# A decoder step on one core: the second MLP tile's relu, square and split issued behind the next pair's first copy

## Chip, core and metric

The kernel runs on one NeuronCore of one Trainium2 chip. The time is the device time of one execution in microseconds (us); of several executions the median is given. The engines are called PE (the matrix engine; PEld its weight loads), DVE (the vector engine), ACT (the scalar engine), POOL and SP (which issues the loads and stores). Each engine works through its own list of instructions in the order in which the program issued them, and waits where an instruction needs another engine's result.

## What is computed

One layer of a hybrid decoder for 512 prompt rows and 8 sample rows together, T = 520 columns in the kernel's transposed layout, all in fp32. The part that matters here is the MLP at its end and the final norm:

```python
u2 = rmsnorm(x, norm2_g) * (1 + sc2) + sh2
hmid = jnp.square(jax.nn.relu(u2 @ w_mlp1))
x = x + g2 * (hmid @ w_mlp2)
...
y_prompt = rmsnorm(yp, norm_f_g)
y_sample = rmsnorm(ys, norm_f_g)
```

The model width is 1024, the MLP's inner width 4096. Everything ahead of it (modulation, input projection, short convolution, state-space scan, output projections) is the same in both kernels.

## The kernel before

**Split products.** Each fp32 operand is written as a high and a low part (hi and lo for activations, wh and wl for weights), and a product is the sum of three matmuls (hi by wh, lo by wh, hi by wl). ACT makes the high part by a copy (`a_copy`, L140), and DVE the low part by a subtraction (`tt`, L128) that needs the copy. All matmuls stand at L143.

**Three groups of pairs.** The first of four quarters of `w_mlp1` is done plainly. In the other three quarters the output tiles (128 rows by T columns each) are made two at a time by `seven` (L1337): with the tokens and the 1024 inputs in halves, a Strassen-like scheme needs seven products instead of eight. A quarter has four such pairs (below pair 1 to pair 4 of a group), and after them come the windows of `w_mlp2` for that quarter, the first two by `two` (L1320), the others by `one` (L1306). The last two windows of the kernel have their own code.

**A pair.** The products p0 to p6 have 12 matmuls each and go to three accumulation banks in the order y, x, w, y, x, w, x. A bank is written again by a later product, so that what must be read of it in between has to be read first. `after(p)` (L1349) issues this reading: behind p0 ACT copies y into `s1` (the first half of tile `su`); behind p1 and p2 DVE adds into `u2_` (the second half of `su`) and `s15` (shown as `s`); behind p3 ACT writes relu of y into the first half of the first output tile `r0`; behind p4 DVE writes half of the second output tile `r1`; behind p5 DVE writes the rest of `r0`, and `squares` (relu, square, copy to hi) issues three ACT instructions on it; behind p6 DVE writes the rest of `r1`, then makes lo of `r0` (`m1_lo`, L790), and `squares` follows on `r1`. Both output tiles appear as `relu` in rows of the profile. What is put into the list `later` is issued in the next pair, in `two` after its first product.

**Weights of a pair.** `split_s` (L292) makes four pairs of wh and wl per pair of tiles, t = 0 to 3, from a loaded weight tile wt and from sums of its quarters, `ss`, that DVE adds first. wh of the sum at t = 2 is issued ahead of p0, its wl ahead of p1; t = 3 ahead of p2 and p3; t = 0 and 1 of the next pair ahead of p4 to p6. So on ACT the two copies from `ss` stand ahead of the copy of y.

**The final norm.** In the last quarter `m2_evac` (L803) finishes x tile by tile: DVE adds the product into `x` (rs, rs, then L131 and a copy at L706), ACT and DVE add its square, and `finish_tile` (L856) transposes the tile on PE (`pt`, `pts`) and multiplies the transposes by the norm's weights on DVE (five `yo` instructions a tile). The place of `finish_tile` is set by `at(q, w, ...)` and `run`: behind quarter q of window w. `mid` is 1 and `end` is 3.

Of the kernel before, what the change touches and what calls it, by code (L numbers as in the profile page):

```python
# [72 lines left out]
def tile_hybrid_step(  # L73
# [32 lines left out]
    def act(name, dtype=F32):  # L106
        return ap.tile([P, SLOT], dtype, name=nm(name), tag="act", bufs=NSLOT)
# [7 lines left out]
    def aux(name):  # L115
        return pp.tile([P, 512], F32, name=nm(name), tag="aux", bufs=4)
# [10 lines left out]
    def tt(out, in0, in1, op):  # L127
        V.tensor_tensor(out=out, in0=in0, in1=in1, op=op)  # L128
# [10 lines left out]
    def a_copy(out, in_, func=AF.Copy, **kw):  # L139
        S.activation(out=out, in_=in_, func=func, **kw)  # L140

    def mm(out, lhsT, rhs, start=True, stop=True, **kw):
        PE.matmul(out, lhsT=lhsT, rhs=rhs, start=start, stop=stop, **kw)  # L143
# [105 lines left out]
    hooks, mid, end = {}, 1, 3  # L249
# [99 lines left out]
    def at(q, w, fn, *args):  # L349
        hooks.setdefault(4 * w + q, []).append((fn, args))  # L350

    def run(w, q):
        while 4 * w + q in hooks:
            for fn, args in sorted(hooks.pop(4 * w + q), key=lambda h: PLAN["order"].get(h[0].__name__, 0)):
                fn(*args)
# [273 lines left out]
    def add_square(acc, t, first, n=T):  # L629
        d = acc if first else act("sqt")  # L630
        a_copy(d[:, 0:n], t[:, 0:n], AF.Square)
        if not first:
            tt(acc[:, 0:n], acc[:, 0:n], d[:, 0:n], ALU.add)
# [67 lines left out]
    def residual(x_, xo, ps, prm, o):  # L701
        t = small([P, NS], "rs")
        tt(t, ps[:, 1, NP - TH:TH], msm(prm, o), ALU.mult)
        tt(t, t, xo[:, NP:T], ALU.add)
        stt(halves(x_[:, 0:T]), ps[:, :, 0:TH], mp(prm, o), halves(xo[:, 0:T]))
        V.tensor_copy(out=x_[:, NP:T], in_=t)  # L706
# [83 lines left out]
    def m1_lo(r, hi, lo):  # L790
        tt(lo[:, 0:T], r[:, 0:T], hi.bitcast(F32)[:, 0:T], ALU.subtract)
        hm.append((hi, lo))
# [10 lines left out]
    def m2_evac(ps, w, o, half):  # L803
        residual(x2[o], x2[o], ps, 5, o)
        if half:
            if o == 0:
                sqf.insert(0, act("sqf"))
            add_square(sqf[0], x2[o], o == 0)
            if o == KT - 3:
                V.memset(vf, 1.0)  # L810
                at(end, w + 1, row_means, sqf, 1.0 / D, vf)
            at(mid if o else end, w + 1, finish_tile, o)

    sqf = []
    vf = const([P, 5], "vf")
# [100 lines left out]
    for f in range(4):  # L916
        for q in range(8):
            if f and q % 2 == 0:
                pairs.add(len(wins))
            win("m1", 0, 1024 * f + 256 * (q // 2), q % 2, lambda: u2, None if f else m1_evac, n1=SLOT - TH)  # L920
        twos.add(len(wins))
        for k in range(KT):
            win("m2", D * f, 256 * (k // 2), k % 2, lambda f=f: hm[8 * f:8 * f + 8],
                lambda ps, w, k=k, f=f: m2_evac(ps, w, k, f == 3))
# [95 lines left out]
    def splits_to(n, whole=True):  # L1020
        while state["split"] < len(units) and state["split"] <= n:
            u_ = units[state["split"]]
            split_w(*u_) if len(u_) == 1 else split_s(*u_)
            state["split"] += 1
        while whole and rests:
            rests.pop(0)()
# [273 lines left out]
    later = []  # L1300

    def evac(n):
        if wins[n][3]:
            wins[n][3](ps_of.pop(n), n)
# [32 lines left out]
    def seven(n):  # L1337
        y, x, w = (aux(z)[:, 0:TH] for z in ("yb", "xb", "wb"))
        banks = (y, x, w, y, x, w, x)
        su, s15, r0, r1 = act("su"), act("s15"), act("relu"), act("relu")  # L1340
        s1, u2_ = su[:, 0:TH], su[:, TH:T]
        hl = [(act("hi", F32R), act("lo", F32R)) for _ in range(2)]

        def squares(r, hi, c0):
            a_copy(r[:, c0:T], r[:, c0:T], AF.Relu)
            a_copy(r[:, 0:T], r[:, 0:T], AF.Square)
            a_copy(hi[:, 0:T], r[:, 0:T])

        def after(p):  # L1349
            if p == 0:  # L1350
                a_copy(s1, y)
                while later:
                    later.pop(0)()
                evac(n - 1)
            elif p == 1:
                tt(u2_, x, s1, ALU.add)
            elif p == 2:
                tt(s15[:, 0:TH], w, s1, ALU.add)
            elif p == 3:
                a_copy(r0[:, 0:TH], y, AF.Relu)  # L1360
            elif p == 4:
                tt(r1[:, TH:T], x, s15[:, 0:TH], ALU.add)
            elif p == 5:
                tt(r0[:, TH:T], w, u2_, ALU.add)
                squares(r0, hl[0][0], TH)
            else:
                tt(r1[:, 0:TH], x, s1, ALU.add)
                m1_lo(r0, *hl[0])
                squares(r1, hl[1][0], 0)
                later.append(lambda: m1_lo(r1, *hl[1]))  # L1370

        for p in range(7):
            splits_to(unit_of[n] + p // 2 + 2, p % 2 == 1)
            (hi, lo), c = splits[n, p // 2], 4 * (p % 2)
            for k in range(4):
                xh, xl = terms[p][k]
                for i, (w_, x_) in enumerate(((hi, xh), (hi, xl), (lo, xh))):
                    mm(banks[p], w_[:, c + k, :], x_, p < 3 and k == 0 and i == 0, k == 3 and i == 2,
                       skip_group_check=True)
            after(p)  # L1380
            run(n + p // 4, p % 4)
        splits_to(unit_of[n] + 5)
        run(n + 1, 3)
# [61 lines left out]
```

## Time and profile before

| | |
|---|---|
| median of 3 runs | 1161.29 us (1161.14 to 1161.82) |
| the profiled execution's own time | 1163.04 us |
| its span in the profile | 1161.3 us |
| PE busy | 1128.1 us |
| DVE busy | 809.0 us |
| ACT busy | 497.5 us |
| four pairs and what follows them until the next group | 872.60 to 962.60, 962.60 to 1052.50 |
| the third group and the end | 1052.50 to 1161.3 |

The span is what the profile shows between the first and the last instruction; the profiled execution took 1.7 us more around it. A row of the timeline gives the start, the length, the engine, the line, the operation with its output and inputs, and in brackets how long the engine stood idle ahead of it and which instruction ended that.

### The profile page before, as it was taken

The numbers are of one execution on the slowest core, as the hardware profiler recorded it, in microseconds if no ns is written. First come the engines' busy times: TensorE is split into PE (matmuls) and PEld (weight loads), VectorE is DVE, ScalarE is ACT, GpSimd is POOL, SyncE is SP. The second block draws the span as 40 slices with busy tenths as digits, with TensorE's granted clock in tenths as the row PEclk, the third lists the DMA queues.
The fourth block names the chain that finished last, engine by engine and source line by source line (L and its number), as shares of the span: only waits on it lengthen the run. The fifth ranks groups of instructions, "written<-read, shape, count | busy, mean of one in ns | idle before, by whom it ended". The sixth has DMA issues, their size and how long they took to land.

```text
span 1161.3 us, 22937 instructions
## 1 busy us (share of the span) xinstructions
PE 1128.1 (97%) x9554; PEld 1092.7 (94%) x9554; DVE 809.0 (70%) x1566; ACT 497.5 (43%) x780; POOL 46.1 (4%) x85
## 2 busy tenths in 40 slices
PE   6999999999999999999999999999999999999997
PEld 5798999999998888999999999999999999999996
DVE  5677888678888587888567334578777647657764
ACT  5456555455552222234443222345536515524622
POOL 3001111011110000000000000003000000000000
PEclk9999999999999999999999999999999999999999
DMA  9924333333348996567563243332222332332302
GB/s 280 326 74 132 114 115 96 94 112 114 114 147 292 324 329 199 178 187 212 171 230 101 95 165 124 114 124 97 81 96 73 109 110 73 109 110 73 104 7 74
DMA packets 137747, 164.96 MB, mean 142 GB/s; under 512 B 7144, under 2 KB 107961, under 8 KB 137636
## 3 DMA queue, kind: packets, MB, share of 16 engines
q1 hardware_dynamic: 137116, 162.85, 42.9%
q8 instruction: 75, 1.23, 0.4%
q0 software_dynamic: 528, 0.66, 0.2%
q14 instruction: 28, 0.23, 0.1%
HBM read 145.26 MB, written 18.45 MB: 141 GB/s over the span
## 4 chain that ended last, share of the span: by engine, by line
PE 83%; ACT 6%; DVE 6%; DMA 3%; issue 1%; SPq 1%; ACTq 0%; DVEq 0%
PE ps L143 72%; DMA wa<-in_w_ada_dram 2%; ACT wh L140 2%; DVE wl L128 2%; ACT relu L140 2%; PE xb L143 1%; PE pada L143 1%; PE pyd L143 1%; PE pst L143 1%; PE pyo L143 1%; PE yb L143 1%; ACT hi L140 1%; PE wb L143 1%; DVE cv L131 1%; DVE ss L128 1%
## 5 line engine op out<-in xcount | busy, mean ns | idle before, releaser
L143 PE MATMUL ps<-hi,wh 128*128 128x260 f32 (+2 forms) x2432 | 501.7, 286 | 2.4 <-ACT cv L140 1.1
L143 PE MATMUL ps<-lo,wh 128*128 128x260 f32 (+2 forms) x2432 | 493.3, 283 | 1.7 <-DVE lo L128 1.4
L143 PE MATMUL ps<-hi,wl 128*128 128x260 f32 (+2 forms) x2432 | 491.0, 282 | 0.0
L143 PEld LDWEIGHTS ps<-hi,wh 128*128 128x128 f32 x2432 | 375.2, 188 | 18.1 <-issue 13.6
L143 PEld LDWEIGHTS ps<-lo,wh 128*128 128x128 f32 x2432 | 376.5, 188 | 3.3 <-DVE lo L128 3.3
L143 PEld LDWEIGHTS ps<-hi,wl 128*128 128x128 f32 x2432 | 376.0, 188 | 0.0
L140 ACT ACTIVATE wh<-wt 128x1024 fp32r<-128x1024 f32 (+1 forms) x191 | 183.1, 960 | 318.3 <-PE ps L143 301.9
L128 DVE TENSOR_TENSOR wl<-wt,wh 128x1024 fp32r<-128x1024 f32 (+1 forms) x191 | 210.4, 1103 | 66.2 <-ACT wh L140 66.2
L131 DVE SCALAR_TENSOR_TENSOR cv<-raw,par,cv 128x511 f32<-128x511 f32 (+2 forms) x72 | 54.0, 750 | 10.9 <-ACT cv L140 9.0
L128 DVE TENSOR_TENSOR rs<-ps,mod 128x8 f32<-128x8 f32 x40 | 6.6, 164 | 62.4 <-PE ps L143 62.4
L140 ACT ACTIVATE wh<-ss 128x512 fp32r<-128x512 f32 x48 | 28.7, 621 | 31.7 <-PE ps L143 26.0
L143 PE MATMUL xb<-hi,wl 128*128 128x260 f32 x144 | 40.8, 283 | 0.0
L143 PE MATMUL xb<-hi,wh 128*128 128x260 f32 x144 | 40.7, 283 | 0.0
L143 PE MATMUL xb<-lo,wh 128*128 128x260 f32 x144 | 40.5, 282 | 0.0
L140 ACT ACTIVATE relu<-relu 128x520 f32<-128x520 f32 (+2 forms) x56 | 29.4, 525 | 20.0 <-DVE relu L128 19.2
L425 POOL TENSOR_SCALAR_AFFINE_SELECT seg<-seg 128x512 f32<-128x512 f32 x32 | 24.9, 801 | 299.6 <-DVE seg L128 243.9
L143 PE MATMUL yb<-hi,wh 128*128 128x260 f32 x96 | 28.1, 293 | 8.2 <-ACT su L140 8.2
L140 ACT ACT_TABLE_LOAD x27 | 34.6, 1283 | 2.9 <-DVE cv L131 1.7
L140 ACT ACTIVATE cv<-cv 128x520 f32<-128x520 f32 x24 | 15.3, 639 | 43.1 <-DVE cv L131 43.1
L128 DVE TENSOR_TENSOR wl<-ss,wh 128x512 fp32r<-128x512 f32 x48 | 31.8, 683 | 0.0
L143 PE MATMUL pada<-wa,cT 128*32 128x128 f32 (+1 forms) x384 | 29.0, 400 | 1.1 <-DMA wa<-in_w_ada_dram 0.9
L131 DVE SCALAR_TENSOR_TENSOR x<-ps,mod,x 128x520 f32<-128x520 f32 (+1 forms) x34 | 24.7, 727 | 5.7 <-PE ps L143 4.6
(312 smaller groups left out, 1332.9 us busy)
## 6 DMA issues: line engine op xcount, KB each, us to landing
wt<-in_w_in_dram SPq DMA_DIRECT2D x38, 1024.0 KB
wt<-in_w_mlp_dram SPq DMA_DIRECT2D x32, 1024.0 KB
wa<-in_w_ada_dram SPq DMA_DIRECT2D x96, 256.0 KB
acb<-ascr SPq DMA_DIRECT2D x32, 256.0 KB
hn<-in_state_ssm_dram SPq DMA_DIRECT2D x32, 256.0 KB
out_dram<-hn SPq DMA_DIRECT2D x32, 256.0 KB
wt<-in_w_b_out_dram SPq DMA_DIRECT2D x8, 1024.0 KB
gscr<-sg SPq DMA_DIRECT2D x16, 260.0 KB
```

The source lines that it names most:

```text
L128: V.tensor_tensor(out=out, in0=in0, in1=in1, op=op)
L131: V.scalar_tensor_tensor(out=out, in0=in0, scalar=scalar, in1=in1, op0=op0, op1=op1)
L140: S.activation(out=out, in_=in_, func=func, **kw)
L143: PE.matmul(out, lhsT=lhsT, rhs=rhs, start=start, stop=stop, **kw)
L425: G.affine_select(out=sv, in_=sv, pattern=[[0, NC], [1, P]], compare_op=ALU.is_ge, fill=-1e30, base=0, channel_multiplier=-1)
```

## The change

In `seven` the relu, the square and the copy to hi of the second output tile are no longer issued at the end of their pair. They go into `later`, and the next pair issues them behind its copy of y (`s1`). The matching `m1_lo` moves from behind p0 of the next pair to behind p2. In `two`, which follows pair 4, both are still issued behind the first product. In `m2_evac` the transposes of the first output tile (o = 0) move from the end of window w + 1 to the middle of window w + 2, where those of o = 1 already stand.

```diff
@@ m2_evac
-            at(mid if o else end, w + 1, finish_tile, o)
+            at(mid, w + (1 if o else 2), finish_tile, o)
@@ seven: after(p)
             if p == 0:
                 a_copy(s1, y)
-                while later:
+                if later:
                     later.pop(0)()
                 evac(n - 1)
             elif p == 1:
                 tt(u2_, x, s1, ALU.add)
             elif p == 2:
                 tt(s15[:, 0:TH], w, s1, ALU.add)
+                while later:
+                    later.pop(0)()
...
             else:
                 tt(r1[:, 0:TH], x, s1, ALU.add)
                 m1_lo(r0, *hl[0])
-                squares(r1, hl[1][0], 0)
+                later.append(lambda: squares(r1, hl[1][0], 0))
                 later.append(lambda: m1_lo(r1, *hl[1]))
```

On ACT, at the seam of pair 2 and pair 3 of the first group, this stood before. The two `wh<-` rows at the top are t = 1 of pair 3, the relu row of 520 columns is relu and square of the second tile of pair 2:

```order
L140 ACTIVATE wh_10825<-ss_10786 128x512
L140 ACTIVATE wh_10825<-wt_10434 128x512
L140 ACTIVATE relu_10714<-relu_10714 128x520 x2
L140 ACTIVATE hi_10717<-relu_10714 128x520
L140 ACTIVATE wh_10865<-ss_10861 128x512
L140 ACTIVATE wh_10865<-ss_10863 128x512
L140 ACTIVATE su_10853<-yb_10850 128x260
L140 ACTIVATE wh_10898<-wt_10434 128x512
```

and this stands now:

```order
L140 ACTIVATE wh_10825<-ss_10786 128x512
L140 ACTIVATE wh_10825<-wt_10434 128x512
L140 ACTIVATE wh_10862<-ss_10858 128x512
L140 ACTIVATE wh_10862<-ss_10860 128x512
L140 ACTIVATE su_10850<-yb_10847 128x260
L140 ACTIVATE relu_10711<-relu_10711 128x520 x2
L140 ACTIVATE hi_10714<-relu_10711 128x520
L140 ACTIVATE wh_10897<-wt_10434 128x512
```

Relu, square and hi have moved behind three instructions, the two copies from `ss` and the copy of y.

On DVE at the same seam (the two sums `ss` for t = 2, then what follows them) this stood before:

```order
L128 TENSOR_TENSOR ss_10861<-wt_10434 128x512
L128 TENSOR_TENSOR ss_10863<-wt_10434,ss_10788 128x512
L128 TENSOR_TENSOR lo_10718<-relu_10714,hi_10717 128x520
L128 TENSOR_TENSOR wl_10866<-ss_10861,wh_10865 128x512
L128 TENSOR_TENSOR wl_10866<-ss_10863,wh_10865 128x512
L128 TENSOR_TENSOR su_10853<-xb_10851,su_10853 128x260
L128 TENSOR_TENSOR s_1406_10854<-wb_10852,su_10853 128x260
L128 TENSOR_TENSOR wl_10899<-wt_10434,wh_10898 128x512
```

and this stands now:

```order
L128 TENSOR_TENSOR ss_10858<-wt_10434 128x512
L128 TENSOR_TENSOR ss_10860<-wt_10434,ss_10788 128x512
L128 TENSOR_TENSOR wl_10863<-ss_10858,wh_10862 128x512
L128 TENSOR_TENSOR wl_10863<-ss_10860,wh_10862 128x512
L128 TENSOR_TENSOR su_10850<-xb_10848,su_10850 128x260
L128 TENSOR_TENSOR s_1406_10851<-wb_10849,su_10850 128x260
L128 TENSOR_TENSOR lo_10715<-relu_10711,hi_10714 128x520
L128 TENSOR_TENSOR wl_10898<-wt_10434,wh_10897 128x512
```

The lo of the second tile has moved behind four instructions and stands now right ahead of the wl of t = 3; the set of instructions is the same.

On DVE in the last quarter (x_8879 is tile o = 0, x_8953 is o = 1) this stood before:

```order
L128 TENSOR_TENSOR wl_13305<-wt_12928,wh_13304 128x1024
L128 TENSOR_TENSOR yo_13320<-pt_13325,gbc_9771 128x128
L128 TENSOR_TENSOR yo_13321<-pt_13325,gbc_9771 128x128
L128 TENSOR_TENSOR yo_13322<-pt_13325,gbc_9771 128x128
L128 TENSOR_TENSOR yo_13323<-pt_13325,gbc_9771 128x128
L128 TENSOR_TENSOR yo_13324<-pts_13326,gbc_9771 8x128
L128 TENSOR_TENSOR rs_13353<-ps_13248,mod_5769 128x8
L128 TENSOR_TENSOR rs_13353<-rs_13353,x_1134_8953 128x8
L131 SCALAR_TENSOR_TENSOR x_1134_8953<-ps_13248,mod_5769,x_1134_8953 128x520
```

and this stands now:

```order
L128 TENSOR_TENSOR wl_13305<-wt_12925,wh_13304 128x1024
L128 TENSOR_TENSOR rs_13336<-ps_13248,mod_5769 128x8
L128 TENSOR_TENSOR rs_13336<-rs_13336,x_1134_8953 128x8
L131 SCALAR_TENSOR_TENSOR x_1134_8953<-ps_13248,mod_5769,x_1134_8953 128x520
```

The five `yo` of the first tile have moved behind the finishing of x of the second; on PE the first tile's five transposes now stand right ahead of the second's.

## Rows read from the trace of the kernel before

**Rows 1.** The page, part 1: busy us (share), instructions.
```profile
PE 1128.1 (97%) x9554; PEld 1092.7 (94%) x9554; DVE 809.0 (70%) x1566; ACT 497.5 (43%) x780; POOL 46.1 (4%) x85
```

**Rows 2.** What PE waited for: us in total, times, longest.
```profile
PE yb L143 <- ACT su L140: 8.2, 9, 0.9
...
PE pt L864 <- DVE x L131: 1.8, 2, 1.5
```

**Rows 3.** Stretches: length, busy PE, PEld, DVE, ACT, POOL, clock, DMA.
```profile
872.60:916.55 43.95, 41.21 (x340) 40.59 (x339) 35.28 (x66) 28.17 (x53) 0.00 (x0) 1.00 0.28 95
916.55:962.60 46.05, 46.05 (x385) 45.96 (x385) 23.57 (x46) 12.26 (x17) 0.00 (x0) 1.00 0.29 94
```

**Rows 4.** Timeline of PE: first matmuls of p0 and p3, pair 3.
```profile
893.88 0.28 PE L143 MATMUL yb<-hi,wh 128*128 128x260 f32 x1
...
899.27 0.39 PE L143 MATMUL yb<-hi,wh 128*128 128x260 f32 x1 [0.92 <-ACT su L140]
```

**Rows 5.** Timeline of DVE from pair 2's end through pair 3 into pair 4.
```profile
892.78 0.42 DVE L128 TENSOR_TENSOR relu<-wb,su 128x260 f32<-128x260 f32 x1
...
895.03 0.70 DVE L128 TENSOR_TENSOR lo<-relu,hi 128x520 fp32r<-128x520 f32 x1 [0.52 <-ACT hi L140]
...
896.85 0.68 DVE L128 TENSOR_TENSOR ss<-wt 128x512 f32<-128x512 f32 x1
897.45 0.68 DVE L128 TENSOR_TENSOR ss<-wt,ss 128x512 f32<-128x512 f32 x1
898.05 0.69 DVE L128 TENSOR_TENSOR lo<-relu,hi 128x520 fp32r<-128x520 f32 x1
898.67 1.28 DVE L128 TENSOR_TENSOR wl<-ss,wh 128x512 fp32r<-128x512 f32 x2
899.87 0.42 DVE L128 TENSOR_TENSOR su<-xb,su 128x260 f32<-128x260 f32 x1
...
900.54 0.68 DVE L128 TENSOR_TENSOR wl<-wt,wh 128x512 fp32r<-128x512 f32 x1
...
904.00 0.42 DVE L128 TENSOR_TENSOR relu<-wb,su 128x260 f32<-128x260 f32 x1
...
913.72 0.43 DVE L128 TENSOR_TENSOR relu<-xb,s 128x260 f32<-128x260 f32 x1 [1.27 <-PE xb L143]
```

**Rows 6.** Timeline of ACT at the seam of pairs 2 and 3.
```profile
894.35 0.64 ACT L140 ACTIVATE hi<-relu 128x520 fp32r<-128x520 f32 x1
...
895.94 1.29 ACT L140 ACTIVATE relu<-relu 128x520 f32<-128x520 f32 x2
897.27 0.64 ACT L140 ACTIVATE hi<-relu 128x520 fp32r<-128x520 f32 x1
897.82 1.13 ACT L140 ACTIVATE wh<-ss 128x512 fp32r<-128x512 f32 x2
898.85 0.36 ACT L140 ACTIVATE su<-yb 128x260 f32<-128x260 f32 x1
```

**Rows 7.** The chain that ended last: start, us, what; pair 4 from p3, then `two`.
```profile
910.50 1.73 PE yb L143 x12
...
916.55 3.48 PE ps L143 x29
```

**Rows 8.** Timeline of PE where the second tile's transposes wait.
```profile
1110.95 0.41 PE L143 MATMUL ps<-hi,wl 128*128 128x260 f32 x2
1112.84 0.66 PE L864 MATMUL pt<-ident,x 128*128 128x128 f32 x4 [1.48 <-DVE x L131]
...
1113.36 0.48 PE L143 MATMUL ps<-hi,wh 128*128 128x260 f32 x2
```

**Rows 9.** Timeline of DVE in the same stretch.
```profile
1110.65 0.88 DVE L128 TENSOR_TENSOR yo<-pt,gbc 128x128 f32<-128x128 f32 x4
...
1111.64 0.14 DVE L128 TENSOR_TENSOR rs<-ps,mod 128x8 f32<-128x8 f32 x1
```

## The prediction

> **What bounds the kernel now.** I read the page first: PE is busy for 97% of the span, DVE for 70%, ACT for 43% [rows 1]. So only time in which PE stands still can be won, and the waits of PE say where that is: the largest entry is nine waits for the copy of y, `su`, 8.2 us together [rows 2]. Three groups with three seams each make nine. The table of stretches shows the same: a group of four pairs takes 43.95 us with PE busy for 41.21, the `w_mlp2` windows behind it take 46.05 and PE is busy for all of them [rows 3]. What is lost in the pairs is therefore not caught up later, and what is won there is kept.
>
> Then the timelines of one seam, to see who sets the pace. PE starts p0 of pair 3 at 893.88 and p3 at 899.27 [rows 4]. A product takes (916.55 - 910.50 - 1.73) / 3 = 1.44 us [rows 7], so p3 was due at 893.88 + 3 x 1.44 = 898.20 and came 1.07 us late, behind `su`.
>
> PE waits, but it is not the engine that sets the period. DVE works from lo of `r0` at 895.03 to the relu row of p5 at 904.00 without one idle gap, sixteen instructions, of which I show some [rows 5]; that is 8.97 us. The remaining 2.25 us, from that relu row (892.78) to lo of `r0` (895.03), is the way over ACT: relu, square and hi of `r0`, for whose end DVE waits 0.52 us [rows 5]. Together 904.00 - 892.78 = 11.22 us, the period of the pairs in the middle. PE needs 7 x 1.44 = 10.08 for a pair. So the middle pairs run on a ring of DVE work and ACT's three instructions on `r0`; PE's wait for `su` is where PE is held back to this period. Only in pair 4, where no `ss` of a next pair is made, does DVE catch up: its sum behind p4 waits 1.27 us for PE [rows 5]. From there PE's p3 sets the end of the group.
>
> **The change at a seam, step by step.** I count from S, the start of the first `ss` for t = 2 (896.85 in pair 3). Before, the second `ss` starts at S + 0.60, lo of `r1` at S + 1.20, the two wl at S + 1.82, `u2_` at S + 3.02, wl of t = 3 at S + 3.69 (900.54) [rows 5]. On ACT relu and square of `r1` start at S - 0.91 and take 1.33 to hi, hi starts at S + 0.42, the two wh from `ss` at S + 0.97, `su` at S + 2.00, and PE's p3 at S + 2.42 [rows 4, 6]. DVE had lo of `r1` ready to go: its hi had ended at S + 1.06.
>
> Now ACT reaches the two wh from `ss` first, and is there too early: it is past hi of `r0` and the wh of t = 1 at 895.94, S - 0.91 [rows 6], and the sums are not made yet. A hand-over between ACT and DVE costs 0.04 (hi of `r0` ends at 894.99, its lo starts at 895.03) [rows 5, 6]. So wh of the first sum starts at S + 0.68 + 0.04 = 0.72, that of the second at S + 0.60 + 0.68 + 0.04 = 1.32. Half of the 1.03 from 897.82 to 898.85 is 0.52, so `su` starts at S + 1.84 instead of 2.00 [rows 6]. **PE's p3 comes 0.16 us earlier, not 1.07.** The removed 1.88 us of ACT work (895.94 to 897.82) mostly gives way to a wait for DVE's sums.
>
> Relu and square of `r1` follow `su`, 0.36 - 0.09 = 0.27 behind its start (ACT's instructions without a wait overlap by 0.09: 897.27 + 0.64 against 897.82), at S + 2.11. hi starts 1.33 later, at S + 3.44, and ends at S + 4.08 [rows 6]. lo of `r1` starts at S + 4.12. It takes 0.62 to the next instruction (898.05 to 898.67), and wl of t = 3 starts at S + 4.74 instead of S + 3.69 [rows 5]. **DVE loses 1.05 us at each seam.** Two wl, `u2_` and `s15` end at about S + 3.3, since lo of `r1` is gone from ahead of them; DVE then stands for some 0.8 us in front of lo, with wl of t = 3, the next pair's `ss`, the sum behind p4 and everything up to p5's relu queued behind it. No work covers this: the same sixteen instructions lie between lo of `r0` and p5's relu, and the ring is now 11.22 + 1.05 = 12.27 us.
>
> **Sum over a group.** Pair 1 has no predecessor and does not change. The seams of pairs 1 and 2 and of pairs 2 and 3 delay the next pair's S by 1.05 each. In pair 4 p3 comes 2 x 1.05 - 0.16 = 1.94 us later. There DVE is 3 x 1.05 = 3.15 late against PE's 1.94, 1.21 more, and it waited 1.27 for PE: the third loss just disappears in that wait. From p3 to the first product of `two` PE needs the same four products, 910.50 to 916.55 [rows 7]. In `two` the late hi and lo are wanted only with its seventh product of 1.44, some 8 us in, so nothing waits for them. A group is 1.94 us longer, three groups 5.8 us.
>
> **The transposes.** Before, PE ends the first half of the second window at about 1111.2, stands 1.48 us for x of tile o = 1, and starts its transposes at 1112.84 [rows 8]. DVE was late for that x by the five `yo` of tile 0, 1110.65 to 1111.64, 0.99 us [rows 9]. With them behind it, x comes 0.99 earlier, and the transposes start at 1111.85. Tile 0's five transposes (1112.84 to 1113.36 is what five take, 0.52 [rows 8]) are only issued later on PE, so PE reaches the wait at the same time. Gain 0.99 us; the bounds are 0 (if DVE's later work fills it) and the 1.65 from 1111.19 to 1112.84. The two tiles' ten `yo` then stand together, 2 us of DVE in a window of some 6 us, which holds.
>
> **Sum.** +5.8 - 1.0 = +4.8 us. The profiled execution (span 1161.3, own time 1163.04) would become 1166.1 and 1167.8; the median of the runs, 1161.29, becomes **1166.1 us**, 0.4% slower. About 0.2% (2.3 us) is what a measurement of this kernel tells from no change. Bounds: with 0.95 a seam, 0.3 won at p3 and 1.65 at the transposes it is 3 x 1.6 - 1.65 = +3.2; with 1.2 a seam, nothing won at p3 and nothing at the transposes it is 3 x 2.4 = +7.2. So 1164.4 to 1168.5 for this case.
>
> **Rivals.**
> - *Faster: the wait of PE closes.* If the sums `ss` were there when ACT comes to them, `su` could follow the end of p0 at once, and the nine late starts of p3, 1.07 each, would go: -9.6 - 1.0, about 1150.7 us. For it speaks that PE is 97% busy and that its largest wait is exactly this one. It decides from the point where the second sum ends by about 897.2 (p3's due time 898.20 less 0.06 and 0.36 for `su`, 0.52 for the wh, 0.04 for the hand-over); it ends at 897.45 + 0.68 = 898.13 [rows 5]. Against it, too: the ring of 11.22 holds no instruction that the change removes. The Trainium skill (Perfetto Trace Analysis, Optimization Strategy) advises to take the most-contended engine, find its gaps, see what they wait for and make that start sooner; by it `su` is to start sooner, and the nine gaps are won back. The trace agrees on the gaps, 8.2 us in nine waits [rows 2], and on nothing beyond them. Chance 0.06.
> - *No change: lo of `r1` does not wait.* If hi were ready when DVE gets there, at S + 3.3, the ring keeps 11.22, and only 3 x 0.16 + 1.0 is won: 1159.8 us. hi would have to end 0.8 us sooner than S + 4.08, though every step behind `su` is one that the rows time. Chance 0.11.
> - *Much slower: further waits add to the ring or to PE.* PE gets new waits: p6 for the sum behind p4, p2 of the next pair for wl of t = 1, each with a restart of up to 1.73 - 1.44 = 0.29 [rows 7]. They cost only from the point where p5 ends after DVE has come to its relu row; p3 starts 0.16 sooner and that row 1.05 later, both from S, so PE has 1.2 us more room than before. Or the clock of PE, 1.00 in these stretches [rows 3], drops. A further 0.5 a seam gives 1161.3 + 4.8 + 4.5 = about 1170.6. Chance 0.07.
>
> **How the numbers follow.** The forecast has 0.76: the DVE ring is read without a gap and the new wait is a sum of seven timed steps. It gives the time. The range, 1162.0 to 1169.0, holds it and the edges of its neighbours; the cases at 1159.8, 1150.7 and most of the one at 1170.6 are left out, under 0.2. Slower by over 0.2%: 0.76 + 0.07, less 0.03 for a forecast case that ends below 1163.6, so 0.80. Faster: 0.06 and a little of the second rival, 0.08. The rest, 0.12, is within 0.2%.
>
> **What the changed profile would show.** DVE's lo of the second tile waits for ACT's hi at each of the nine seams, about 0.8 us. ACT's two wh wait for `ss`. The period from lo of `r0` to lo of `r0` is about 12.27. PE's waits for `su` shrink in pair 2 (by 0.16) and new ones appear in front of wl or relu. The first group takes about 45.9 us instead of 43.95. The transposes of tile 1 wait some 0.5 us instead of 1.48. I am wrong if the period stays at 11.22, if lo of `r1` finds its hi ready, or if the group gets shorter.

## The result and the profile after

The changed kernel takes 1167.36 us (median of four runs, 1166.5 to 1168.9) against 1161.55 for the kernel before in runs beside it: ratio 1.0051, 95% interval 1.0033 to 1.0068. The forecast was 1166.1 in a range of 1162.0 to 1169.0. The profiled execution has a span of 1165.6 us, 4.3 more than before, and a time of 1167.36.

The page's first part and the waits of PE (engine, line, what it waited for: us in total, times, longest), to be held against [rows 1, 2]:

```profile
PE 1130.2 (97%) x9554; PEld 1095.8 (94%) x9554; DVE 811.3 (70%) x1566; ACT 497.8 (43%) x780; POOL 46.1 (4%) x85
```

```profile
PE yb L143 <- ACT su L140: 9.9, 9, 1.3
...
PE xb L143 <- DVE relu L128: 2.4, 6, 0.4
...
PE pt L864 <- DVE x L131: 0.8, 2, 0.4
```

The nine waits for `su` are longer in total, though the first of a group is shorter (0.76 us below, 0.90 before), and six new ones stand in front of the x bank (p6, which waits for the sum behind p4). Of the waits in the part that was changed, only that of the transposes shrank. The stretches of the first group and of what follows it, with the columns of [rows 3]:

```profile
871.92:917.63 45.71, 41.64 (x338) 40.66 (x337) 35.92 (x66) 27.96 (x53) 0.00 (x0) 1.00 0.24 80
917.63:963.90 46.27, 46.27 (x387) 46.19 (x386) 23.48 (x46) 12.43 (x17) 0.00 (x0) 1.00 0.33 104
```

The clock is 1.00 as before, and the windows of `w_mlp2` take much the same time. The loss is in the pairs. Its size needs the same bounds on both sides: here the group ends at the first matmul of `two`, while [rows 3] end it at 916.55, which is 0.16 us behind that matmul:

```profile
916.39 0.40 PE L143 MATMUL ps<-hi,wh 128*128 128x260 f32 x2
```

From first matmul to first matmul the group took 916.39 - 872.60 = 43.79 us before, and takes 45.71 now.

DVE at the seam of pairs 1 and 2, to be held against [rows 5]:

```profile
883.11 0.70 DVE L128 TENSOR_TENSOR lo<-relu,hi 128x520 fp32r<-128x520 f32 x1 [0.50 <-ACT hi L140]
...
884.93 0.69 DVE L128 TENSOR_TENSOR ss<-wt 128x512 f32<-128x512 f32 x1
885.53 0.69 DVE L128 TENSOR_TENSOR ss<-wt,ss 128x512 f32<-128x512 f32 x1
886.38 1.29 DVE L128 TENSOR_TENSOR wl<-ss,wh 128x512 fp32r<-128x512 f32 x2 [0.16 <-ACT wh L140]
...
889.06 0.70 DVE L128 TENSOR_TENSOR lo<-relu,hi 128x520 fp32r<-128x520 f32 x1 [0.72 <-ACT hi L140]
889.68 0.68 DVE L128 TENSOR_TENSOR wl<-wt,wh 128x512 fp32r<-128x512 f32 x1
...
895.40 0.70 DVE L128 TENSOR_TENSOR lo<-relu,hi 128x520 fp32r<-128x520 f32 x1 [1.08 <-ACT hi L140]
...
914.96 0.43 DVE L128 TENSOR_TENSOR relu<-xb,s 128x260 f32<-128x260 f32 x1
```

Here S is 884.93. The second row with lo is that of the second tile: it waits 0.72 us for ACT's hi, at S + 4.13, and wl of t = 3 follows at S + 4.75. From lo of `r0` to the next lo of `r0` it is 895.40 - 883.11 = 12.29 us. The last row is the sum behind p4 in pair 4; it waited 1.27 us for PE before and now comes without a wait. ACT at the same seam ([rows 6] before):

```profile
885.71 1.17 ACT L140 ACTIVATE wh<-ss 128x512 fp32r<-128x512 f32 x2 [1.59 <-DVE ss L128]
886.79 0.37 ACT L140 ACTIVATE su<-yb 128x260 f32<-128x260 f32 x1
887.06 1.30 ACT L140 ACTIVATE relu<-relu 128x520 f32<-128x520 f32 x2
888.39 0.64 ACT L140 ACTIVATE hi<-relu 128x520 fp32r<-128x520 f32 x1
```

ACT stands 1.59 us in front of the sums, in the time in which it squared the second tile before; relu, square and hi follow `su`. PE starts p3 and p6 of this pair behind these waits ([rows 4] before):

```profile
887.21 0.39 PE L143 MATMUL yb<-hi,wh 128*128 128x260 f32 x1 [0.76 <-ACT su L140]
...
892.18 0.36 PE L143 MATMUL xb<-hi,wh 128*128 128x260 f32 x1 [0.39 <-DVE relu L128]
```

The transposes in the last quarter, PE and then DVE ([rows 8, 9] before):

```profile
1116.06 0.60 PE L864 MATMUL pt<-ident,x 128*128 128x128 f32 x4
...
1117.16 0.66 PE L864 MATMUL pt<-ident,x 128*128 128x128 f32 x4 [0.40 <-DVE x L131]
```

```profile
1114.81 1.23 DVE L128 TENSOR_TENSOR wl<-wt,wh 128x1024 fp32r<-128x1024 f32 x1 [1.66 <-ACT wh L140]
1115.95 0.16 DVE L128 TENSOR_TENSOR rs<-ps,mod 128x8 f32<-128x8 f32 x1
```

DVE goes from the wl straight to the second tile's rs, and PE waits 0.40 us instead of 1.48. Before, this wl of DVE started 3.33 us ahead of the transposes (1112.84 - 1109.51 [rows 8]), now it is 2.35 us ahead of them:

```profile
1109.51 1.23 DVE L128 TENSOR_TENSOR wl<-wt,wh 128x1024 fp32r<-128x1024 f32 x1 [1.65 <-ACT wh L140]
```

**The account.** By the chain that ended last, the three groups grew by 1.93, 1.94 and 1.95 us (45.72, 45.73, 45.72 against 43.79, 43.79, 43.77), the windows behind the first two by 0.23 together, the end from the third `two` on shrank by 1.06, and the first group began 0.69 sooner: 5.82 + 0.23 - 1.06 - 0.69 = 4.30, the span's 4.3. The 0.69 lie ahead of the first group, where the two kernels are the same; one wait of PE there (`prb` for DVE's `rst`) was 1.5 us before and is 0.5 now, and in the other runs it lies between 0.5 and 2.0. The medians lie 5.8 apart because the profiled execution of before was itself 1.5 us above its median.

### The profile page after: what moved, and what is told of

Same layout as the page of the kernel before. It is cut to its first block, busy times and chain, and to the rows that moved or that the text cites. A ratio compares the mean times of both kernels' runs of the same rounds, so it can differ in the third digit from the quotient of the medians.

```text
span 1165.6 us, 22924 instructions
## 1 busy us (share of the span) xinstructions
PE 1130.2 (97%) x9554; PEld 1095.8 (94%) x9554; DVE 811.3 (70%) x1566; ACT 497.8 (43%) x780; POOL 46.1 (4%) x85
## 4 chain that ended last, share of the span: by engine, by line
PE 83%; DVE 8%; ACT 5%; issue 1%; ACTq 0%; DVEq 0%
PE ps L143 72%; DVE wl L128 3%; PE pada L143 2%; PE xb L143 1%; ACT relu L140 1%; PE pyd L143 1%; PE pst L143 1%; DVE lo L128 1%; PE pyo L143 1%; PE yb L143 1%; ACT wh L140 1%; DVE ss L128 1%; ACT hi L140 1%; PE wb L143 1%; DVE cv L131 1%
## 5 line engine op out<-in xcount | busy, mean ns | idle before, releaser
L128 DVE TENSOR_TENSOR lo<-relu,hi 128x520 fp32r<-128x520 f32 x32 | 22.4, 700 | 21.0 <-ACT hi L140 20.7
L143 PEld LDWEIGHTS xb<-hi,wh 128*128 128x128 f32 x144 | 27.1, 188 | 3.4 <-issue 3.4
```

## The experiments

Eleven kernels, each timed in five rounds against the kernel before on the same chip. Its median there stands with each result.

**1 and 2. The two halves of the change apart.** First the pairs' part alone: the changed kernel with the old place of the first transposes.

```diff
-            at(mid, w + (1 if o else 2), finish_tile, o)
+            at(mid if o else end, w + 1, finish_tile, o)
```

> Only the seam part of the change, with the transposes of the first output tile where they were before. If the loss is the new wait of DVE at the seams: the ring from lo of r0 to lo of r0 is about 12.3 us as in the changed kernel, each group 1.9 us longer, about +5.8 us, 1167.3 us; PE waits 1.5 us for x ahead of the second tile's transposes as before. If the transposes' place were what costs: within 1 us of the kernel before, 1161.5 us.

Measured 1168.75 against 1163.55, ratio 1.0052 (1.0038 to 1.0066). The wait for the transposes is back at 1.8 us, the ring is 12.29. Then the same line, with the signs exchanged, in the kernel before:

> Only the transposes part, with the pairs as before. If the five yo ahead of x were what PE waited for: PE's wait there falls from 1.5 us to about 0.5 and the kernel gains 1.0 us, about 1160.5 us. If the place of the transposes does not matter or costs: 1161.5 us or more.

Measured 1162.10 against 1163.55, ratio 0.9987 (0.9977 to 0.9997). The whole loss is in the pairs; the transposes win about a microsecond. By the medians the two add up to +5.20 - 1.45 = +3.75, by the ratios to +6.0 - 1.5 = +4.5, where the whole change had +4.3 between profiles and +5.8 between medians.

**3. Is it the place of lo, or ACT's list?** In the changed kernel lo of the second tile moves further back, from behind p2 to behind p4, so that it can't hold up wl of t = 3.

```diff
             elif p == 2:
                 tt(s15[:, 0:TH], w, s1, ALU.add)
-                while later:
-                    later.pop(0)()
...
             elif p == 4:
                 tt(r1[:, TH:T], x, s15[:, 0:TH], ALU.add)
+                while later:
+                    later.pop(0)()
```

> The changed kernel with lo of r1 one step later, behind p4 instead of p2, so that its hi is long there. Theory one (the wait of lo is the whole loss): without it the ring goes back to 11.2 us and the transposes' gain stays, about 1160.5 us. Theory two (ACT's late end of relu, square and hi holds up everything behind them on ACT too): wh of t = 3 stands behind hi on ACT and ends at S + 4.6, so wl of t = 3 waits in lo's place until S + 4.65, and lo's own 0.62 us then comes on top of it. Ring 11.22 + 0.96 + 0.62 = 12.8 us, each group 3.0 us longer than before, about 1169.5 us.

Measured 1171.08 against 1163.55, ratio 1.0069 (1.0056 to 1.0083). DVE:

```profile
890.72 0.69 DVE L128 TENSOR_TENSOR wl<-wt,wh 128x512 fp32r<-128x512 f32 x1 [1.23 <-ACT wh L140]
...
892.99 0.69 DVE L128 TENSOR_TENSOR lo<-relu,hi 128x520 fp32r<-128x520 f32 x1
```

lo no longer waits, but wl of t = 3 does: its wh stands on ACT behind the relu, square and hi that were moved. So lo's wait in the changed kernel is only the first to show what holds DVE up, which is ACT's list. lo itself, 0.6 us, then comes on top behind the wait, and the ring is 12.82 (884.25, 897.07, 909.88).

**4. The opposite half: only lo moves.** In the kernel before, relu, square and hi stay, and lo goes behind p2 as in the change.

```diff
             if p == 0:
                 a_copy(s1, y)
-                while later:
-                    later.pop(0)()
...
             elif p == 2:
                 tt(s15[:, 0:TH], w, s1, ALU.add)
+                while later:
+                    later.pop(0)()
```

> From the kernel before: lo of r1 alone moves behind p2; relu, square and hi of r1 stay at the end of their pair, and the transposes as before. hi is ready long before, so lo waits for nothing. If only the wait for hi costs: no change, 1161.5 us. If lo also was cover for DVE's wait for wh of the sums (ACT ends the first wh at S + 1.59, DVE is there at S + 1.20 without lo): DVE stands 0.43 us at each seam, ring 11.65, each group 0.9 us longer, about +2.6 us, 1164.1 us.

Measured 1166.07 against 1163.55, ratio 1.0028 (1.0018 to 1.0038), ring 11.65 (884.85, 896.50, 908.16). DVE:

```profile
888.29 1.29 DVE L128 TENSOR_TENSOR wl<-ss,wh 128x512 fp32r<-128x512 f32 x2 [0.33 <-ACT wh L140]
...
890.17 0.69 DVE L128 TENSOR_TENSOR lo<-relu,hi 128x520 fp32r<-128x520 f32 x1
```

lo was also the work that DVE did while ACT copied the sums to wh. Away from there it leaves a wait, although nothing on DVE became more.

**5 to 7. The sums on POOL.** POOL is idle in the pairs, and the sums of DVE are what ACT now waits for. The first sum of each two goes to POOL, in the order of before (5), in the changed order (6), and with the squares behind p2 and lo behind p4 (7).

```diff
-        def total(i, x, y, op):
+        def total(i, x, y, op, eng=V):
...
-            tt(sums[i], x, y, op)
+            eng.tensor_tensor(out=sums[i], in0=x, in1=y, op=op)
...
-            total(1, a21, a22, ALU.add)
+            total(1, a21, a22, ALU.add, G)
...
-            total(3, a11, a21, ALU.subtract)
+            total(3, a11, a21, ALU.subtract, G)
```

> From the kernel before, in its order: the first of the two sums at t = 0 and at t = 2 is made on POOL, which is idle here, so DVE has two instructions of 512 columns fewer a pair (0.72 + 0.60 us). If DVE's ring alone holds the pairs at 11.22 us, it falls to 9.9 and PE's 10.08 becomes the bound: about 2.3 us a group, -7 us. If there is a second ring of nearly the same length, over ACT and PE (p3 to the end of p5 4.65 us, the relu row 0.45, relu and square and hi of r0, two wh, relu and square and hi of r1, two wh, su: 5.62 us, hand-over 0.42, together 11.14 us), the pairs stay at 11.1 us and at most 0.5 us is won.

> The changed kernel with the same two sums on POOL. DVE's ring then holds lo's wait as before but is 1.31 us shorter than 12.28, about 10.97 us; ACT's and PE's ring has lost relu, square and hi of r1 and is some 9.3 us. p3 stands 3.5 us behind lo of r0 instead of 4.25. Together a group is 1.3 us shorter than before, with the transposes about -4.9 us. If POOL's sums are slow or hold up DVE, the ring is longer than 11.2 and nothing is won.

> As the kernel before this one, but relu, square and hi of r1 behind p2, so that wh of t = 3 stands ahead of them on ACT, and lo of r1 behind p4. Then lo finds its hi and wl of t = 3 its wh: DVE's ring is about 10.1 us, as long as PE's seven products. Each group 3.0 us or more shorter than before, with the transposes about -10 us. If DVE's waits were not the point but the amount of work on DVE, it does as well as the kernel before this one, -5 us.

Measured against 1162.48: 1164.65, ratio 1.0018 (1.0009 to 1.0027); 1162.43, ratio 0.9999 (0.9990 to 1.0007); 1164.94, ratio 1.0016 (1.0007 to 1.0025). So 5 is slower than the kernel before, which neither of its two cases had; 6 has no gain on the kernel before, though the changed kernel, from which it differs only in the sums, was at 1.0051; and the gain of 7 did not come either. One cause stands in the rows of 6, DVE and POOL:

```profile
883.69 1.83 DVE L128 TENSOR_TENSOR lo<-relu,hi 128x520 fp32r<-128x520 f32 x1 [0.50 <-ACT hi L140]
...
887.25 2.62 DVE L128 TENSOR_TENSOR wl<-ss,wh 128x512 fp32r<-128x512 f32 x2
...
896.06 0.70 DVE L128 TENSOR_TENSOR lo<-relu,hi 128x520 fp32r<-128x520 f32 x1 [0.75 <-ACT hi L140]
...
907.03 0.70 DVE L128 TENSOR_TENSOR lo<-relu,hi 128x520 fp32r<-128x520 f32 x1 [0.98 <-ACT hi L140]
```

```profile
883.66 1.30 POOL L298 TENSOR_TENSOR ss<-wt 128x512 f32<-128x512 f32 x1 [10.53 <-DMA wt<-in_w_mlp_dram]
888.00 1.31 POOL L298 TENSOR_TENSOR ss<-wt 128x512 f32<-128x512 f32 x1 [3.04 <-DVE wl L128]
```

While POOL adds, a DVE instruction of 0.70 us takes 1.83, and two of 1.29 together take 2.62. In this pair DVE loses more beside POOL than it is relieved of, and the ring is 12.37 (883.69 to 896.06). The Trainium skill (Perfetto Trace Analysis, Optimizing Scalar/DVE Operations) warns that GPSIMD and DVE share an SBUF read port, so that moving work between them might not help; these rows agree. Which port it is no run here shows. But POOL runs ahead: of a group's eight sums only these two fall beside the ring, and in the next pair, where POOL does nothing, the ring is 10.97 (896.06 to 907.03), just what was expected. The 1.4 us between the two pairs are about what a group of 6 falls short of the expected gain of 1.3.

In 5 there are also two instructions less on DVE where POOL does not disturb it, and the ring there is still 11.24 (897.10 to 908.34). That asked for another path as long as DVE's. It is in DVE's waits there:

```profile
897.10 0.70 DVE L128 TENSOR_TENSOR lo<-relu,hi 128x520 fp32r<-128x520 f32 x1 [0.50 <-ACT hi L140]
...
900.02 0.70 DVE L128 TENSOR_TENSOR lo<-relu,hi 128x520 fp32r<-128x520 f32 x1 [0.41 <-ACT hi L140]
...
904.54 0.43 DVE L128 TENSOR_TENSOR relu<-xb,s 128x260 f32<-128x260 f32 x1 [0.74 <-PE xb L143]
```

lo of the second tile waits for ACT, and the sum behind p4 for PE. In 7 the first of these waits is gone and the second is 0.91. Its ring is 12.69 beside POOL and 11.10 without it (883.07, 895.76, 906.86), where 10.1 was expected: POOL costs 1.6 us in one pair of a group, and the other 1.0 stays where POOL does nothing, with the sum behind p4 waiting for PE.

**8. The order of 7 without POOL.** The squares go behind p2, lo behind p4, the sums stay on DVE.

```diff
             if p == 0:
                 a_copy(s1, y)
-                if later:
-                    later.pop(0)()
...
             elif p == 2:
                 tt(s15[:, 0:TH], w, s1, ALU.add)
-                while later:
+                if later:
                     later.pop(0)()
...
             elif p == 4:
                 tt(r1[:, TH:T], x, s15[:, 0:TH], ALU.add)
+                while later:
+                    later.pop(0)()
```

> The order of the kernel before this one without POOL: relu, square and hi of r1 behind p2, lo behind p4, all sums on DVE. Neither lo nor wl of t = 3 waits for ACT; only DVE's wait for the first wh (0.16 us) is new against the kernel before. Ring 11.4 us, a group 0.2 us longer, with the transposes about -0.3 us: no change to be told from the kernel before, and 5 to 6 us faster than the changed kernel. If moving relu, square and hi costs by itself, wherever lo stands: as slow as the changed kernel.

Measured 1164.72 against 1162.48, ratio 1.0018 (1.0009 to 1.0026), ring 11.73 (895.94 to 907.67): faster than the changed kernel, but slower than the kernel before, where a ring of 11.4 and no change were expected. DVE:

```profile
903.26 0.43 DVE L128 TENSOR_TENSOR relu<-xb,s 128x260 f32<-128x260 f32 x1 [0.15 <-PE xb L143]
903.61 0.69 DVE L128 TENSOR_TENSOR lo<-relu,hi 128x520 fp32r<-128x520 f32 x1
```

wl of t = 3 and lo wait no more, so relu, square and hi at this place cost nothing by themselves. But the sum behind p4 waits for PE, whose p3 and p4 follow `su`, and `su` follows the sums; lo stands behind that sum and is added to this path. The sums are still what everything starts from. So they have to come sooner.

**9 to 11. The sums a step ahead.** The two sums for t = 2 need only the loaded weight tile. They are issued on DVE in the pair before, right ahead of the three ACT instructions on `r0`, for whose end DVE waits in any case.

```diff
+    def early_sums(n):
+        if n not in pairs:
+            return
+        early.add(n)
...
+        for i, x, y in ((3, a11, a21), (4, a12, sums[2])):
+            sums[i] = act("ss")[:, 0:512].rearrange("p (k n) -> p k n", n=P)
+            tt(sums[i], x, y, ALU.subtract)
...
-        elif t == 2:
+        elif t == 2 and n not in early:
...
             elif p == 5:
                 tt(r0[:, TH:T], w, u2_, ALU.add)
+                early_sums(n + 2)
                 squares(r0, hl[0][0], TH)
```

Number 9 is the kernel before with this, 10 the changed kernel with this, and 11 has besides this the squares behind p2 and lo just ahead of the sum behind p4.

> From the kernel before: DVE makes the two sums for t = 2 right behind the relu row of p5 of the pair ahead, where it waits for ACT anyway (2.25 us with one instruction of 0.34 in it), instead of behind lo of r0 and the two wl. DVE's ring loses 1.2 us of 11.22. If DVE's ring alone holds the pairs: the period falls to PE's 10.1, about 2.5 us a group, -7 us. If the path over ACT and PE (relu, square and hi of r1 ahead of the copy of y, then p3 and p4 or p5) is as long: the period stays at 11.1 to 11.2 us and at most 0.6 us is won.

> The changed kernel with the same early sums. ACT now finds the sums when it comes to them, su starts 1.95 us behind lo of r0, and p3 starts when PE gets there. lo of r1 still waits (0.5 us) for its hi. DVE's ring about 10.6 us, a group about 3 us shorter than before, with the transposes about -10 us: both halves together win what neither wins alone. If relu, square and hi behind su are what costs: as slow as the changed kernel, +5 us.

> As the kernel before this one, with relu, square and hi of r1 behind wh of t = 3 on ACT, and lo of r1 just ahead of the sum behind p4 on DVE, where hi is ready. DVE's ring 10.0 us, so PE's seven products (10.08) are the bound: about 3.3 us a group, with the transposes about -11 us. If lo's wait is of no account by now: as fast as the kernel before this one.

Measured against 1162.92: 1162.68, ratio 1.0005 (0.9996 to 1.0013); **1153.25, ratio 0.9917 (0.9904 to 0.9931); 1151.16, ratio 0.9895 (0.9880 to 0.9910).** DVE in 9, 10 and 11, from one lo of `r0` to the next, with lo of the second tile between them (for 9 also the relu rows of p5 and the sum behind p4):

```profile
881.27 0.42 DVE L128 TENSOR_TENSOR relu<-wb,su 128x260 f32<-128x260 f32 x1
...
883.52 0.70 DVE L128 TENSOR_TENSOR lo<-relu,hi 128x520 fp32r<-128x520 f32 x1 [0.29 <-ACT hi L140]
...
886.43 0.70 DVE L128 TENSOR_TENSOR lo<-relu,hi 128x520 fp32r<-128x520 f32 x1 [1.01 <-ACT hi L140]
...
890.98 0.43 DVE L128 TENSOR_TENSOR relu<-xb,s 128x260 f32<-128x260 f32 x1
...
892.52 0.42 DVE L128 TENSOR_TENSOR relu<-wb,su 128x260 f32<-128x260 f32 x1
...
894.78 0.70 DVE L128 TENSOR_TENSOR lo<-relu,hi 128x520 fp32r<-128x520 f32 x1 [0.29 <-ACT hi L140]
```

```profile
883.67 0.70 DVE L128 TENSOR_TENSOR lo<-relu,hi 128x520 fp32r<-128x520 f32 x1 [0.29 <-ACT hi L140]
...
887.89 0.70 DVE L128 TENSOR_TENSOR lo<-relu,hi 128x520 fp32r<-128x520 f32 x1 [0.41 <-ACT hi L140]
...
894.24 0.70 DVE L128 TENSOR_TENSOR lo<-relu,hi 128x520 fp32r<-128x520 f32 x1 [0.29 <-ACT hi L140]
```

```profile
884.26 0.70 DVE L128 TENSOR_TENSOR lo<-relu,hi 128x520 fp32r<-128x520 f32 x1 [0.29 <-ACT hi L140]
...
889.91 0.69 DVE L128 TENSOR_TENSOR lo<-relu,hi 128x520 fp32r<-128x520 f32 x1
...
894.34 0.70 DVE L128 TENSOR_TENSOR lo<-relu,hi 128x520 fp32r<-128x520 f32 x1 [0.29 <-ACT hi L140]
```

In 9 the two sums are gone from the ring, and 1.01 of their 1.20 us come back as a wait of lo for ACT; the ring is still 11.26. From lo of `r0` to lo of the second tile it takes 886.43 - 883.52 = 2.91 us, where the kernel before took 898.05 - 895.03 = 3.02 [rows 5]; the 0.11 won there are lost again at the sum behind p4, which has to follow PE. The copy of y in 9, and the sum behind p4 in the kernel before:

```profile
887.35 0.36 ACT L140 ACTIVATE su<-yb 128x260 f32<-128x260 f32 x1
```

```profile
902.47 0.42 DVE L128 TENSOR_TENSOR relu<-xb,s 128x260 f32<-128x260 f32 x1
```

So in 9 the pairs run on a second ring, over ACT and PE. From the relu row of p5 over ACT's three instructions on `r0`, two wh, its three on the second tile and the two wh from `ss` to `su` it is 887.35 - 881.27 = 6.08 us; over p3 and p4 to the sum behind p4, 890.98 - 887.35 = 3.63; over two wl to the next relu row of p5, 892.52 - 890.98 = 1.54. In the kernel before the same three steps took 898.85 - 892.78 = 6.07, 902.47 - 898.85 = 3.62 and 904.00 - 902.47 = 1.53 [rows 5, 6]. It had two rings of the same length: one over DVE's sums, one over ACT's relu, square and hi of the second tile. In 10 both have been shortened, lo waits 0.41 for the hi behind `su`, and the ring is 10.57. In 11 that wait is gone too, the ring is 10.08, the 7 x 1.44 that PE needs, and the table of stretches has PE without a gap:

```profile
870.00:910.00 40.00, 40.00 (x335) 40.00 (x335) 34.60 (x66) 26.71 (x51) 0.00 (x0) 1.00 0.26 80
```

## Why the prediction was right, and where it was short

- **The bound** held: the pairs run on a ring over DVE and ACT, and PE's waits for `su` only follow it. They grew from 8.2 to 9.9 us in the changed kernel, since the ring grew.
- **The seam** held to 0.02 us at each step. Counted from S, `su` started at 1.86 (forecast 1.84), p3 at 2.28 (2.26), hi at 3.46 (3.44), lo at 4.13 (4.12), wl of t = 3 at 4.75 (4.74). The ring is 12.29 (12.27). DVE's wait for the first wh, 0.16, was not in the sum; it falls into the time in which lo would have waited anyway, so that lo waits 0.72 instead of some 0.8. Experiment 3 adds that lo's wait could not have been dodged by putting lo elsewhere.
- **The group** is 1.93 to 1.95 us longer (1.94), and the third loss disappears in pair 4's wait of 1.27, as reckoned. The 45.9 us forecast for the first group were 1.94 on top of 43.95, which holds 0.16 of `two`; measured are 45.71.
- **The transposes** won 0.98 between the wl ahead of them and their start (2.35 against 3.33; forecast 0.99), and PE waits 0.40 (some 0.5).
- **The sum**, +4.8, lies between the profiles' +4.3 and the medians' +5.8, inside the interval of +3.8 to +7.9 that the ratio gives. The 1.3 us by which the median missed the forecast is not more than the scatter of the runs.
- **The rival "faster"** was priced at 1150.7 on the condition that the sums are there when ACT comes to them. They were not. Experiment 10 fulfils the condition and gives 1153.25 against 1162.92, a gain of 9.7 of the 10.6 reckoned; 11 gives 11.8. The Trainium skill's advice to make what a gap waits for start sooner (Perfetto Trace Analysis, Optimization Strategy) failed in the change, because there the start of `su` hung on DVE's sums; with the sums early too, the trace agrees, and 10 has no wait for `su` left.
- **Short** was the statement that the ring of 11.22 holds no instruction that the change removes. It is true of DVE's ring, but the second ring, over ACT and PE (experiment 9), was just as long and holds relu, square and hi of the second tile. The chain that ended last, from which [rows 7] were taken, goes this way at the same seam:

```profile
896.04 0.54 ACT relu L140
...
897.82 1.13 ACT wh L140 x2
```

The forecast did not need the second ring: the change made DVE's longer and this one shorter, and the longer one sets the period. But whoever had reckoned from DVE's ring alone what less work on DVE brings would have been wrong, as the expectation of 7 was (a ring of 10.1, measured 11.10 where POOL does nothing). With less on DVE ahead of it, the sum behind p4 waits for PE in 5, 7 and 8 (0.74, 0.91 and 0.15 us).

## What to carry to other kernels

A kernel can run on several rings of the same length at once. Taking work out of one of them wins nothing (9: 1.0005), moving it out of the other may lose when the first has to wait for it at its new place (the change: 1.0051), and both together win 0.8 to 1.1% (10 and 11). So before moving an instruction, time every way that joins at the place where the engines meet, and ask what the instruction was hiding where it stood (4: lo hid a wait of 0.33 us). And the largest wait of the busiest engine may be only where another ring shows: here it was 97% busy, and what had to be moved as well were two sums on an engine that was 70% busy.

## What was not expected of the hardware

A POOL addition of 128 x 512 fp32 elements takes 1.3 us in most cases (1.28 to 2.36 in 6), about twice DVE's 0.69, and stretches DVE's instruction beside it from 0.70 to 1.83 us, although POOL works on other tiles. Under way together, DVE lost 1.13 us to 1.30 us of POOL's work. Handing DVE's additions to an idle POOL lost time in the order of before (5: 1.0018), changed nothing with the squares and lo moved back (7: 1.0016, against 1.0018 for 8 without POOL), and in the changed order won back what the change had lost (6: 0.9999, against 1.0051).
